# Scores of 64 rows filled up, gates summed in two parts, queries and keys turned

## The chip, the cores and the metric

The kernel runs on one core of one Trainium2 chip. The metric is device time in microseconds (us) of one execution; three runs are given, and their median counts. Every time in this document that is said to come from the profile belongs to one further execution, which a hardware profiler recorded. The engines are TensorE (PE; its weight loads are listed as PEld), VectorE (DVE), ScalarE (ACT), GpSimd (POOL) and SyncE (SP), whose queue issues nearly all transfers.

## The reference

256 tokens of width 2048 pass through three layers, all in fp32.

- **Retention** (8 heads, 256 wide queries and keys, 512 wide values): `h = rmsnorm(x) * (1 + scale) + shift`, where shift, scale and gate are `silu(c) @ ada_w + ada_b`; `proj = h @ w_in` (2048 x 12288) gives q, k, v and g; q and k are rotated by the positions (half-split rotary embedding over all 256 columns); scores `q k^T` times a decay, times v, normalised per head, times `silu(g)`, `@ w_out`; `x = x + gate * y`.
- **Latent attention** (16 heads): again shift, scale and gate; low-rank q and kv; each head's score is a product over 128 plain columns plus one over 64 rotated columns, whose key is the same for all heads; softmax, values, gate.
- **Mixed attention and experts**: 16 forgetting heads of 64 columns, whose score gets a difference of cumulated log gates added; 16 dilated heads of 64 columns, of which 16 are rotated; then a PEER layer with 16384 experts: each token's top experts weigh a down and an up projection.

## The kernel before

**Products in three parts.** A big fp32 product is done as three products of type fp32r, whose elements are a high part `h` and a low part `l = x - h`: high times high, high times low, low times high, all summed in PSUM. `split` (L169) makes the parts: ACT copies to the high part (L170), DVE subtracts (L171). Weights come by `weights` (L173): one DMA of 1 MB into one of three `raw` buffers, then two half tiles, each split into one of four pairs of buffers. Small products (scores, values, the gates' sums) are plain fp32, which PE runs as two records each.

**Projections.** `proj_steps` (L228) computes 256 tokens x 512 columns: for each of the 16 blocks of 128 input columns and for each half `tb` of the tokens, the activations (128 x 128) are the stationary operand and the weights (128 x 512) the moving one; three matmuls (L241 to L243). After each half weight tile it yields, and `proj` calls `tick` (L199), which advances background tasks at set rates: attention of the head pair before, transposes, the adaptive sums of the next layer. So the program order is fixed by Python; the framework's planner then orders the instructions of each engine by its own model of when operands are ready, and that order is fixed on the chip.

**Retention.** `begin` (L550) starts before all of the normalised input is there: ten column blocks are done in four quarters `g` of the input columns and summed up in SBUF, those of q and k of the first head pair among them. `angles` (L390) makes the tables of cosines and sines, tokens on the partitions. Then head pairs 1 to 3 follow (`project`, L606). The evacuation of q and k (L633) rotates the PSUM result with `rope` (L519: four DVE products, two POOL sums), and since the score needs q and k with their columns on the partitions, four PE transposes per 128 tokens follow (L640), and an ACT copy (L641). `attend` (L656) runs later, beside the next projections.

**Gates.** `ada_gate` (L478) computes four gate blocks of 512 columns for a layer: DVE sums 16 weight rows per partition into `acc` (L432, four DMA loads of 1 MB; one load is one step of the task), and PE sums over the partitions and spreads the result to all of them:

```
            nc.tensor.matmul(p, self.ones, acc, start=True, stop=False)
            nc.tensor.matmul(p, self.ones[0:1, :], bias[0:1, :], start=False, stop=True)
```

The task runs at 0.3 (layer 0) and 0.32 (layer 1) steps per tick; `output` (L703) calls `upto`, which runs the task until the gates that its column block needs are done.

**Scores.** `softmax_v` (L325) does one head: for each half of the queries the score products (L337), mask and maximum, exponential, transposes (L352), values (L358 to L360). In the latent heads a score is two products, the second over 64 rows (L857): the rotated parts of two heads lie in rows 0 to 63 and 64 to 127 of `qrT`, and `krT` holds the key twice. In the mixed attention the forgetting heads have 66 rows (64 and two for the cumulated gates), the dilated heads 64 (`kk`, L977 and L1028).

Of the kernel before, what the change touches and what calls it, by code (L numbers as in the profile page):

```python
# [36 lines left out]
C_ID, C_ONE, C_TRI, C_IOTA, C_CAUSAL, C_DIL, C_COS2, C_SIN2, C_INVF, C_END = (  # L37
    0, 128, 256, 384, 512, 768, 1152, 1168, 1184, 1312)
# [8 lines left out]
def shape_constants():  # L47
    c = np.zeros((128, C_END), np.float32)
    i = np.arange(128)
    c[:, C_ID:C_ID + 128] = np.eye(128)  # L50
    c[:, C_ONE:C_ONE + 128] = 1.0
    c[:, C_TRI:C_TRI + 128] = i[:, None] <= i[None, :]
    c[:, C_IOTA:C_IOTA + 128] = i[None, :]
    c[:, C_CAUSAL + 128:C_CAUSAL + 256] = np.where(i[None, :] <= i[:, None], 0.0, NEG)

    def dil(q, k):
        d = q[:, None] - k[None, :]
        n = ((d >= 0) & (d <= 128)).astype(np.int64)
# [11 lines left out]
    c[:, C_INVF:C_INVF + 128] = np.float32(10000.0) ** (-np.arange(0, 256, 2, dtype=np.float32) / np.float32(256))  # L70
# [52 lines left out]
class Net:  # L123
# [131 lines left out]

    def columns_steps(self, out, pool, name, nk, src, gain=None, shift=None, bufs=1, tiles=None, pause=False):
# [108 lines left out]
    def start(self):  # L365
# [19 lines left out]
        self.ones = self.cst[:, C_ONE:C_ONE + 128]  # L385
        nc.scalar.dma_start(self.cst, a["consts"])
# [3 lines left out]
    def angles(self):  # L390

        nc, keep, a = self.nc, self.keep, self.a
        self.cos = keep.tile([128, 2, 128], F32, name="cos")
        self.sin = keep.tile([128, 2, 128], F32, name="sin")
        pi = keep.tile([128, 2], I32, name="posi")
        nc.scalar.dma_start(pi, a["positions"].rearrange("o (b p) -> p (o b)", p=128))
        pf = keep.tile([128, 2], F32, name="posf")
        nc.vector.tensor_copy(pf, pi)
        ang = self.w(256).rearrange("p (b f) -> p b f", b=2)
        for tb in range(2):  # L400
            nc.vector.tensor_scalar(ang[:, tb, :], self.cst[:, C_INVF:C_INVF + 128], pf[:, tb:tb + 1], None,
                                    op0=OP.mult)
        k = self.w(256).rearrange("p (b f) -> p b f", b=2)
# [10 lines left out]
        nc.scalar.activation(self.sin, ang, AF.Sin)  # L414
        nc.vector.scalar_tensor_tensor(k, ang, -1.0, ang, op0=OP.mult, op1=OP.max)
        nc.vector.tensor_scalar(k, k, -1.0, float(np.pi / 2), op0=OP.mult, op1=OP.add)
        nc.scalar.activation(self.cos, k, AF.Sin)
# [60 lines left out]
    def ada_gate(self, layer, G):  # L478

        nc = self.nc  # L480
        for g in range(4):
# [52 lines left out]
    def retention(self):  # L534
# [5 lines left out]
        with self.phase("ret", 8), self.tc.tile_pool(name="ret", bufs=1) as pool:  # L540
# [9 lines left out]
            def begin():  # L550
# [18 lines left out]
                for g in range(4):  # L569
                    ada = self.ada_first(g + 1, A, B, ring, acc) if g < 3 else iter(())  # L570
                    if g == 3:
                        self.angles()
                    for i, (c0, dst) in enumerate(blocks):
# [6 lines left out]
                        for _ in self.proj_steps(ps, hT[g:], 4 * g, 4, w_in, c0, 512):  # L580
                            pass
# [24 lines left out]
            def project(i, between=None):  # L606
# [18 lines left out]
                def product(c0, early, ev):  # L625
                    if early is not None:
                        for tb in range(2):
                            ev(tb, early[:, tb, :])
                    else:
                        self.proj(hT, 0, 16, w_in, c0, 512, ev)  # L630

                for n, dst in enumerate((qT, kT)):
                    def ev(tb, p, dst=dst):  # L633
                        o = self.w()
                        self.rope(p.rearrange("p (h s d) -> p h s d", h=2, s=2),
                                  o.rearrange("p (h s d) -> p h s d", h=2, s=2), 2, 128,
                                  self.cos[:, tb, :], self.sin[:, tb, :])
                        p2 = self.tmp()
                        for j in range(4):
                            nc.tensor.transpose(p2[:, j * 128:j * 128 + 128], o[:, j * 128:j * 128 + 128], self.ident)  # L640
                        nc.scalar.activation(dst[:, :, tb * 128:tb * 128 + 128],  # L641
                                             p2.rearrange("p (k t) -> p k t", k=4), AF.Copy)
                    product(n * 2048 + i * 512, None if qk is None else qk[:, :, n * 512:n * 512 + 512], ev)
                for b in range(2):
                    def ev(tb, p, b=b):
                        nc.scalar.activation(v[:, tb, b * 512:b * 512 + 512], p, AF.Copy)
                    if i > 1:
                        product(4096 + i * 1024 + b * 512, None, ev)
# [91 lines left out]
    def latent(self):  # L740
# [4 lines left out]
        with self.phase("mla", 7), ExitStack() as es:  # L745
# [18 lines left out]
            krT = pool.tile([128, 256], F32, name="krT")  # L764
# [3 lines left out]
            def latents():  # L768
# [18 lines left out]
                nc.scalar.activation(krT, p[:, :256], AF.Copy)  # L787
# [5 lines left out]
            for c0, c1 in ((0, 424), (424, 848), (848, 1272), (1272, 1696), (1696, 2112)):  # L793
                def ev(tb, p, c0=c0, c1=c1):
                    o = max(64 - c0, 0)
                    if o:
                        self.rope(p[:, :64].rearrange("p (h s d) -> p h s d", h=1, s=2), kr[:, tb], 1, 32,
                                  self.cos[:, tb, ::4], self.sin[:, tb, ::4])
# [12 lines left out]
            def project(i):  # L811
# [6 lines left out]
                def evq(tb, p):  # L818
# [5 lines left out]
                              self.cos[:, tb, ::4], self.sin[:, tb, ::4])  # L824
# [20 lines left out]
            def head(i, j):  # L845
# [3 lines left out]
                def done(o, rd):  # L849
                    nc.vector.tensor_scalar(rd, rd, 0.5, None, op0=OP.mult)  # L850
                    for tb in range(2):
# [5 lines left out]
                                (qrT[j * 64:j * 64 + 64, tb * 128:tb * 128 + 128],  # L857
                                 krT[j * 64:j * 64 + 64, :128 * (tb + 1)])],
# [70 lines left out]
    def mixed(self):  # L929
# [3 lines left out]
        with self.phase("mix", 8), self.tc.tile_pool(name="mix", bufs=1) as pool:  # L933
# [41 lines left out]
            def project(n, g, beside=iter(())):  # L975

                kk = 66 if n == "f" else 64  # L977
# [16 lines left out]
                for off in (0, 1024):  # L994
                    def ev(tb, p, off=off):
# [15 lines left out]
                        else:  # L1011
                            nc.scalar.activation(dst[:, 0, :, 16:64], pv[:, :, 16:64], AF.Copy,
# [4 lines left out]
                        for h in range(0, 8, 4):  # L1017
                            p2 = self.tmp()
                            for j in range(4):
                                nc.tensor.transpose(p2[:kk, j * 128:j * 128 + 128], dst[:, 0, h + j, :kk], self.ident)  # L1020
                            nc.scalar.activation(dT[:kk, h:h + 4, tb * 128:tb * 128 + 128],
                                                 p2[:kk, :].rearrange("p (h t) -> p h t", h=4), AF.Copy)
# [3 lines left out]
            def head(n, g, h):  # L1026
                qT, kT, v = st[n, g]
                kk = 66 if n == "f" else 64  # L1028
# [6 lines left out]
                def done(o, rd):  # L1035
# [5 lines left out]
                    lambda tb: [(qT[:kk, h, tb * 128:tb * 128 + 128], kT[:kk, h, :128 * (tb + 1)])],  # L1041
# [538 lines left out]
```

## Time and profile before

| | us |
|---|---|
| median of three runs (3292.64 to 3299.68) | 3298.16 |
| profiled execution, its own time | 3290.79 |
| its span in the trace | 3289.0 |
| PE busy | 3199.2 (97%) |
| PE weight loads busy | 2731.8 (83%) |
| DVE busy | 2366.5 (72%) |
| ACT busy | 1563.5 (48%) |
| POOL busy | 403.9 (12%) |

705.51 MB are moved, 215 GB/s on average. The granted clock of PE is 0.996 over the execution. A matmul's record is longer than its distance to the next one, since matmuls overlap; so the start times in a timeline tell what one costs, and the busy share doesn't.

### The profile page before, as it was taken

The page shows a single profiled execution, that of the slowest core. Times are in us where ns is not written, and L with a number is a line of the kernel's source. Part 1 is how long each engine was busy: PE and PEld are TensorE (multiplying, and loading weights), DVE is VectorE, ACT ScalarE, POOL GpSimd, SP SyncE. Part 2 cuts the span into 40 slices and gives each one's busy share as a digit, 9 for nine tenths or more (in the row PEclk, how much of TensorE's full clock was granted, in tenths as well). Part 3 has the DMA queues.
Part 4 walks back from the last instruction along what each step waited for, and adds up shares of the span by engine and source line. Part 5 has one row for each costly group of instructions (what it writes and reads, how often), then busy time and mean ns, then how long its engine had stood idle before and what let it go on. Part 6 is the DMA issues. An engine that isn't in the chain of part 4 may idle for free.

```text
span 3289.0 us, 46220 instructions
## 1 busy us (share of the span) xinstructions
PE 3199.2 (97%) x17874; PEld 2731.8 (83%) x17874; DVE 2366.5 (72%) x3923; ACT 1563.5 (48%) x2167; POOL 403.9 (12%) x478
## 2 busy tenths in 40 slices
PE   5999999999999999999999999999999999999998
PEld 3777778777788878887787999999888898999987
DVE  6898778778786666455569976999766666566665
ACT  3544444343545546555454444555544444444444
POOL 0001101101000230000000221788000000000000
PEclk9999999999999999999999999999999999999999
DMA  9875677676575334443454456777977755555553
GB/s 343 315 259 204 222 282 293 235 272 255 194 282 202 127 144 171 154 149 135 147 173 152 167 180 212 238 259 248 317 240 240 240 208 204 198 200 192 192 192 141
DMA packets 141532, 705.51 MB, mean 215 GB/s; under 512 B 12664, under 2 KB 45688, under 8 KB 67584
## 3 DMA queue, kind: packets, MB, share of 16 engines
q1 hardware_dynamic: 139152, 696.51, 60.2%
q10 hardware_dynamic: 2160, 6.05, 0.5%
q8 instruction: 140, 2.29, 0.3%
q14 instruction: 80, 0.66, 0.1%
HBM read 676.30 MB, written 26.21 MB: 214 GB/s over the span
## 4 chain that ended last, share of the span: by engine, by line
PE 80%; DVE 10%; DMA 5%; issue 3%; ACT 1%; POOL 1%; POOLq 0%; DVEq 0%; SPq 0%; ACTq 0%
PE acc L241 12%; PE acc L242 12%; PE acc L243 11%; PE acc L1249 7%; PE acc L1251 7%; PE acc L1250 7%; PE tmp L1169 5%; PE tmp L1170 5%; PE tmp L1171 5%; DVE wl L171 3%; PE tmp L337 2%; DVE w L432 1%; PE acc L1171 1%; PE acc L1170 1%; PE acc L1169 1%
## 5 line engine op out<-in xcount | busy, mean ns | idle before, releaser
L171 DVE TENSOR_TENSOR wl<-raw,wh 128x1024 fp32r<-128x1024 f32 (+4 forms) x983 | 1202.3, 1229 | 504.1 <-ACT wh L170 503.0
L170 ACT ACTIVATE wh<-raw 128x1024 fp32r<-128x1024 f32 (+4 forms) x983 | 1017.5, 1043 | 1008.0 <-PE acc L243 383.3
L242 PE MATMUL acc<-wl,hTh 128*128 128x512 f32 (+4 forms) x1536 | 599.7, 391 | 11.1 <-DVE wl L171 11.1
L241 PE MATMUL acc<-wh,hTh 128*128 128x512 f32 (+4 forms) x1536 | 604.2, 396 | 2.1 <-ACT wh L170 2.0
L243 PE MATMUL acc<-wh,hTl 128*128 128x512 f32 (+4 forms) x1536 | 597.6, 389 | 0.7 <-DVE hTl L288 0.7
L1169 PE MATMUL tmp<-hTh,wh 128*128 128x256 f32 x1280 | 360.6, 282 | 0.0
L1170 PE MATMUL tmp<-hTh,wl 128*128 128x256 f32 x1280 | 357.9, 280 | 0.0
L1171 PE MATMUL tmp<-hTl,wh 128*128 128x256 f32 x1280 | 357.3, 279 | 0.0
L242 PEld LDWEIGHTS acc<-wl,hTh 128*128 128x128 f32 x1536 | 290.4, 189 | 74.8 <-DVE wl L171 17.7
L241 PEld LDWEIGHTS acc<-wh,hTh 128*128 128x128 f32 x1536 | 289.6, 189 | 63.6 <-ACT wh L170 4.5
L243 PEld LDWEIGHTS acc<-wh,hTl 128*128 128x128 f32 x1536 | 289.8, 189 | 62.4 <-issue 2.4
L1249 PE MATMUL acc<-wh,Wh 128*128 128x512 f32 x812 | 317.1, 390 | 0.3 <-ACT Wh L170 0.2
L1251 PE MATMUL acc<-wh,Wl 128*128 128x512 f32 x812 | 316.3, 390 | 0.9 <-DVE Wl L171 0.9
L1250 PE MATMUL acc<-wl,Wh 128*128 128x512 f32 x812 | 316.2, 389 | 0.0
L1169 PEld LDWEIGHTS tmp<-hTh,wh 128*128 128x128 f32 x1280 | 240.5, 188 | 0.7
L1170 PEld LDWEIGHTS tmp<-hTh,wl 128*128 128x128 f32 x1280 | 240.0, 188 | 0.8
L1171 PEld LDWEIGHTS tmp<-hTl,wh 128*128 128x128 f32 x1280 | 240.0, 188 | 0.1
L1467 POOL TENSOR_SCALAR oh<-iota,slot 128x128 f16<-128x128 f16 x256 | 209.6, 837 | 167.8 <-DVE iota L1458 87.1
L432 DVE SCALAR_TENSOR_TENSOR w<-raw,cact,w 128x512 f32<-128x512 f32 x240 | 183.1, 763 | 18.3 <-DMA raw<-in_ada_dram 13.7
L160 POOL TENSOR_TENSOR tiny<-tiny,mhalf 128x1 f32<-128x1 f32 (+1 forms) x23 | 17.6, 764 | 1382.5 <-DVE tiny L159 1382.5
L1170 PE MATMUL acc<-hTh,wl 128*128 128x256 f32 x640 | 179.9, 281 | 6.8 <-DVE wl L171 6.8
L1249 PEld LDWEIGHTS acc<-wh,Wh 128*128 128x128 f32 x812 | 152.4, 188 | 33.7 <-DVE x L1258 2.3
(352 smaller groups left out, 5220.2 us busy)
## 6 DMA issues: line engine op xcount, KB each, us to landing
raw<-in_down_dram SPq DMA_DIRECT2D x128, 1024.0 KB, 5.3
raw<-in_up_dram SPq DMA_DIRECT2D x128, 1024.0 KB, 4.9
raw<-in_ret_w_in_dram SPq DMA_DIRECT2D x96, 1024.0 KB, 5.5
raw<-in_ada_dram SPq DMA_DIRECT2D x64, 1024.0 KB, 5.6
raw<-in_w_in_dram SPq DMA_DIRECT2D x44, 1024.0 KB, 4.8
raw<-in_ret_w_out_dram SPq DMA_DIRECT2D x32, 1024.0 KB, 4.8
G<-in_ada_first_dram SPq DMA_DIRECT2D x32, 512.0 KB, 5.1
raw<-in_mla_w_out_dram SPq DMA_DIRECT2D x16, 1024.0 KB, 4.8
```

The costliest lines, as they stand in the source:

```text
L170: self.nc.scalar.activation(h, raw, AF.Copy)
L171: self.nc.vector.tensor_tensor(l, raw, h.bitcast(F32), op=OP.subtract)
L241: nc.tensor.matmul(o, sh, wh[:, j, :], start=(k == 0), stop=False)
L242: nc.tensor.matmul(o, sh, wl[:, j, :], start=False, stop=False)
L243: nc.tensor.matmul(o, sl, wh[:, j, :], start=False, stop=(k == nk - 1))
L432: nc.vector.scalar_tensor_tensor(acc, r, self.cact[:, k:k + 1], acc, op0=OP.mult, op1=OP.add)
L1169: nc.tensor.matmul(o, dh[:, s], hh[:, k % 4, :], start=(k == 0), stop=False)
L1170: nc.tensor.matmul(o, dl[:, s], hh[:, k % 4, :], start=False, stop=False)
L1171: nc.tensor.matmul(o, dh[:, s], hl[:, k % 4, :], start=False, stop=(k == 15))
L1249: nc.tensor.matmul(y[tb][c], Wh[:, s], uh[:, u], start=first, stop=False)
L1250: nc.tensor.matmul(y[tb][c], Wh[:, s], ul[:, u], start=False, stop=False)
L1251: nc.tensor.matmul(y[tb][c], Wl[:, s], uh[:, u], start=False, stop=last)
```

## The change

- **Scores.** `krT` gets one plane per head of a pair, with the key in that head's 64 rows and zeros in the others; the product takes all 128 rows of `qrT`. The dilated heads get two columns of zeros behind their 64, and 66 rows take part everywhere.
- **Gates.** The bias is added to row 0 of `acc`; `acc` is split in a high and a low part, and two fp32r products with a tile of ones follow, one step later. A gate is five steps instead of four, and `output` asks for them so.
- **Queries and keys.** `turned_steps` makes the weights (128 x 128) the stationary operand and the activations (128 x 256 tokens) the moving one, so that q and k arrive with their columns on the partitions: half a head (128 columns) in each half of a PSUM bank. They are rotated straight from there (four DVE products of 512 columns, four POOL sums of 256 per block of two heads) into `qT` and `kT`; the transposes and their copies are gone. `angles` makes tables with the columns on the partitions, and small ones (32 columns) of the old form for the latent layer.

```diff
+    def turned_steps(self, ps, hT, nk, name, c0):
+        nc = self.nc
+        k = 0
+        for k0 in range(hT[0], hT[0] + nk, 4):
+            for wh, wl in self.weights(name, k0, c0):
+                for j in range(2):
+                    hh, hl = (t[:, (k0 + k % 4) % 4, :] for t in hT[1][(k0 + k % 4) // 4])
+                    for c in range(4):
+                        o = ps[c // 2][:, c % 2 * 256:c % 2 * 256 + 256]
+                        sh, sl = (t[:, j, c * 128:c * 128 + 128] for t in (wh, wl))
+                        nc.tensor.matmul(o, sh, hh, start=(k == 0 and c % 2 == 0), stop=False, skip_group_check=True)
+                        nc.tensor.matmul(o, sh, hl, start=False, stop=False, skip_group_check=True)
+                        nc.tensor.matmul(o, sl, hh, start=False, stop=(k == nk - 1 and c % 2 == 1),
+                                         skip_group_check=True)
+                    k += 1
+                yield
...
     def ada_gate(self, layer, G):
...
-            p = self.tmp()
             bias = self.w()
             nc.scalar.dma_start(bias[0:1, :], self.a["ada_b"][layer:layer + 1, c0:c0 + 512])
-            nc.tensor.matmul(p, self.ones, acc, start=True, stop=False)
-            nc.tensor.matmul(p, self.ones[0:1, :], bias[0:1, :], start=False, stop=True)
+            nc.vector.tensor_tensor(acc[0:1, :], acc[0:1, :], bias[0:1, :], op=OP.add)
+            ah, al = (self.w().bitcast(F32R) for _ in range(2))
+            self.split(acc, ah, al)
+            yield
+            p = self.tmp()
+            nc.tensor.matmul(p, self.onesr, ah, start=True, stop=False)
+            nc.tensor.matmul(p, self.onesr, al, start=False, stop=True)
...
-                        for _ in self.proj_steps(ps, hT[g:], 4 * g, 4, w_in, c0, 512):
+                        if i < 2:
+                            steps = self.turned_steps(ps, (4 * g, hT), 4, w_in, c0)
+                        else:
+                            steps = self.proj_steps(ps, hT[g:], 4 * g, 4, w_in, c0, 512)
+                        for _ in steps:
                             pass
...
+                    if qk is None:
+                        ps = [self.acc() for _ in range(2)]
+                        for _ in self.turned_steps(ps, (0, hT), 16, w_in, n * 2048 + i * 512):
+                            self.tick()
+                    for h in range(2):
+                        p = (ps[h] if qk is None else qk[:, h, n * 512:n * 512 + 512]).rearrange(
+                            "p (s t) -> p s t", s=2)
+                        t = [self.w().rearrange("p (s t) -> p s t", s=2) for _ in range(2)]
+                        for o, tab in zip(t, (self.cosT, self.sinT)):
+                            nc.vector.tensor_tensor(o, p, tab[:, None, :].to_broadcast([128, 2, 256]), op=OP.mult)
+                        nc.gpsimd.tensor_tensor(dst[:, 2 * h, :], t[0][:, 0, :], t[1][:, 1, :], op=OP.subtract)
+                        nc.gpsimd.tensor_tensor(dst[:, 2 * h + 1, :], t[0][:, 1, :], t[1][:, 0, :], op=OP.add)
...
-                    self.upto(ada, 4 * cb + 4)
+                    self.upto(ada, 5 * cb + 5)
...
-            krT = pool.tile([128, 256], F32, name="krT")
+            krT = pool.tile([128, 2, 256], F32, name="krT")
+            nc.gpsimd.memset(krT, 0.0)
...
-                nc.scalar.activation(krT, p[:, :256], AF.Copy)
+                for d in range(2):
+                    r = slice(d * 64, d * 64 + 64)
+                    nc.scalar.activation(krT[r, d, :], p[r, :256], AF.Copy)
...
-                                (qrT[j * 64:j * 64 + 64, tb * 128:tb * 128 + 128],
-                                 krT[j * 64:j * 64 + 64, :128 * (tb + 1)])],
+                                (qrT[:, tb * 128:tb * 128 + 128], krT[:, j, :128 * (tb + 1)])],
...
+                            nc.gpsimd.memset(dst[:, 0, :, 64:66], 0.0)
...
-                    lambda tb: [(qT[:kk, h, tb * 128:tb * 128 + 128], kT[:kk, h, :128 * (tb + 1)])],
+                    lambda tb: [(qT[:66, h, tb * 128:tb * 128 + 128], kT[:66, h, :128 * (tb + 1)])],
```

## Rows read from the trace of the kernel before

**Rows 1.** The page's first part: busy us, share of the span, instructions of each engine.
```profile
PE 3199.2 (97%) x17874; PEld 2731.8 (83%) x17874; DVE 2366.5 (72%) x3923; ACT 1563.5 (48%) x2167; POOL 403.9 (12%) x478
```

**Rows 2.** Stretches (us): length, then busy us of each engine; clock, DMA share, GB/s.
```profile
274.00:858.00 584.00, 569.83 (x2480) 446.89 (x2479) 461.49 (x619) 238.63 (x285) 67.21 (x64) 0.99 0.68 250
858.00:1012.00 154.00, 147.61 (x704) 128.75 (x703) 124.05 (x177) 72.33 (x110) 4.48 (x6) 0.98 0.73 264
1012.00:1258.00 246.00, 245.48 (x1259) 200.84 (x1258) 163.66 (x373) 128.48 (x265) 51.76 (x57) 1.00 0.40 136
1258.00:1600.00 342.00, 338.38 (x1711) 273.37 (x1709) 176.52 (x409) 186.73 (x330) 10.33 (x30) 1.00 0.45 157
```

**Rows 3.** PE's waits: line, waited for whom: us in total, times, longest.
```profile
PE acc L242 <- DVE wl L171: 12.6, 14, 3.0
...
PE tmp L640 <- POOL w L530: 10.3, 6, 5.4
```

**Rows 4.** PE's timeline in a projection: start us, us, line, operation, shapes, count.
```profile
270.12 0.40 PE L243 MATMUL acc<-wh,hTl 128*128 128x512 f32 x1
...
284.12 0.40 PE L243 MATMUL acc<-wh,hTl 128*128 128x512 f32 x1
```

**Rows 5.** PE's timeline around a score of 66 rows and one of 64 rows.
```profile
1333.62 0.40 PE L243 MATMUL acc<-wh,hTl 128*128 128x512 f32 x1
1333.86 0.39 PE L337 MATMUL tmp<-qkT,qkT 66*128 66x128 f32 x2
...
1334.32 0.40 PE L242 MATMUL acc<-wl,hTh 128*128 128x512 f32 x1
...
1506.29 0.39 PE L242 MATMUL acc<-wl,hTh 128*128 128x512 f32 x1
1506.61 0.48 PE L337 MATMUL tmp<-qkT,qkT 64*128 64x128 f32 x2
...
1507.37 0.39 PE L241 MATMUL acc<-wh,hTh 128*128 128x512 f32 x1
```

**Rows 6.** Line L337 on PE: count, ns min/median/max, first and last start, forms.
```profile
L337 PE MATMUL tmp<-qkT,qkT x128: 272/375/481, 1333.9 to 1645.2; 66*128 66x128 f32 x32, 66*128 66x256 f32 x32, 64*128 64x128 f32 x32, 64*128 64x256 f32 x32
...
L337 PE MATMUL tmp<-krT,qrT x64: 272/374/480, 1033.0 to 1213.7; 64*128 64x128 f32 x32, 64*128 64x256 f32 x32
```

**Rows 7.** Groups in 274 to 858: busy us, mean ns | idle before, releaser.
```profile
L432 DVE SCALAR_TENSOR_TENSOR w<-raw,cact,w 128x512 f32<-128x512 f32 x180 | 138.1, 767 | 14.9 <-DMA raw<-in_ada_dram 11.5
...
L516 DVE TENSOR_TENSOR w<-acc,G 128x512 f32<-128x512 f32 x30 | 19.6, 683 | 0.8 <-PE acc L243 0.8
...
L528 DVE TENSOR_TENSOR w<-acc,cos 128x256 f32<-128x256 f32 x24 | 9.9, 413 | 0.1
...
L530 POOL TENSOR_TENSOR w<-w 128x256 f32<-128x256 f32 x12 | 9.1, 762 | 42.7 <-DVE w L529 42.7
```

**Rows 8.** PE's timeline at a gate, and line L490 as a whole.
```profile
336.72 1.02 PE L490 MATMUL tmp<-w,cst 128*128 128x512 f32 x2
337.67 1.12 PE L491 MATMUL tmp<-w,cst 1*128 1x512 f32 x2
338.72 1.09 PE L273 MATMUL tmp<-ident,sg 128*128 128x128 f32 x8
...
L490 PE MATMUL tmp<-w,cst x16: 590/592/667, 336.7 to 1003.9; 128*128 128x512 f32 x16
```

**Rows 9.** PE's timeline in the experts' down projection.
```profile
1849.96 0.28 PE L1170 MATMUL acc<-hTh,wl 128*128 128x256 f32 x1
...
1852.78 0.28 PE L1170 MATMUL acc<-hTh,wl 128*128 128x256 f32 x1
```

**Rows 10.** The page's groups: weight loads of the down projection.
```profile
L1169 PEld LDWEIGHTS tmp<-hTh,wh 128*128 128x128 f32 x1280 | 240.5, 188 | 0.7
```

**Rows 11.** PE's timeline at the first head pair's transposes.
```profile
285.05 1.91 PE L640 MATMUL tmp<-ident,w 128*128 128x128 f32 x16
```

**Rows 12.** PE's timeline at the longest wait, and the stretch behind it.
```profile
630.59 0.48 PE L640 MATMUL tmp<-ident,w 128*128 128x128 f32 x1 [5.39 <-POOL w L530]
...
630.00:634.00 4.00, 3.41 (x12) 2.77 (x13) 4.00 (x7) 0.03 (x1) 3.04 (x4) 0.58 0.15 23
```

More of the change, by code (lines that the diff above doesn't have):

```diff
@@ L69, in shape_constants @@
         c[:, C_SIN2 + 8 * b:C_SIN2 + 8 * b + 8] = np.sin(ang[b * 128:b * 128 + 128].astype(np.float64))
-    c[:, C_INVF:C_INVF + 128] = np.float32(10000.0) ** (-np.arange(0, 256, 2, dtype=np.float32) / np.float32(256))
+    freq = np.float32(10000.0) ** (-np.arange(0, 256, 2, dtype=np.float32) / np.float32(256))
+    c[:, C_INVF:C_INVF + 32] = freq[::4]
+    c[:, C_COLF] = freq
     m = np.zeros((128, 8, 384), np.float32)
@@ L385, in start, with angles, trig @@
         self.ones = self.cst[:, C_ONE:C_ONE + 128]
+        self.onesr = keep.tile([128, 128], F32R, name="onesr")
         nc.scalar.dma_start(self.cst, a["consts"])
         nc.vector.tensor_scalar(self.colv[:, V_GN:V_GN + 32], self.colv[:, V_GN:V_GN + 32], 0.5, None, op0=OP.mult)
-    def angles(self):
+    def angles(self, pool):
         nc, keep, a = self.nc, self.keep, self.a
-        self.cos = keep.tile([128, 2, 128], F32, name="cos")
-        self.sin = keep.tile([128, 2, 128], F32, name="sin")
+        self.cosT = pool.tile([128, 256], F32, name="cosT")
+        self.sinT = pool.tile([128, 256], F32, name="sinT")
+        self.cos = keep.tile([128, 2, 32], F32, name="cos")
+        self.sin = keep.tile([128, 2, 32], F32, name="sin")
+        pos = a["positions"]
+        pr = self.w(256).bitcast(I32)
+        nc.scalar.dma_start(pr, bass.AP(tensor=pos.tensor, offset=pos.offset, ap=[[0, 128], [1, 256]]))
+        ang = self.w(256)
+        nc.vector.tensor_copy(ang, pr)
+        nc.vector.tensor_scalar(ang, ang, self.cst[:, C_COLF:C_COLF + 1], None, op0=OP.mult)
+        self.trig(ang, self.cosT, self.sinT, 256)
+        nc.vector.tensor_copy(self.onesr, self.ones)
         pi = keep.tile([128, 2], I32, name="posi")
-        nc.scalar.dma_start(pi, a["positions"].rearrange("o (b p) -> p (o b)", p=128))
+        nc.scalar.dma_start(pi, pos.rearrange("o (b p) -> p (o b)", p=128))
         pf = keep.tile([128, 2], F32, name="posf")
         nc.vector.tensor_copy(pf, pi)
-        ang = self.w(256).rearrange("p (b f) -> p b f", b=2)
+        ang = self.w(64)
         for tb in range(2):
-            nc.vector.tensor_scalar(ang[:, tb, :], self.cst[:, C_INVF:C_INVF + 128], pf[:, tb:tb + 1], None,
-                                    op0=OP.mult)
-        k = self.w(256).rearrange("p (b f) -> p b f", b=2)
+            nc.vector.tensor_scalar(ang[:, tb * 32:tb * 32 + 32], self.cst[:, C_INVF:C_INVF + 32], pf[:, tb:tb + 1],
+                                    None, op0=OP.mult)
+        self.trig(ang, *(t.rearrange("p b f -> p (b f)") for t in (self.cos, self.sin)), 64)
+    def trig(self, ang, cos, sin, n):
+        nc = self.nc
+        k = self.w(n)
         magic = 12582912.0
@@ L623, in project @@
                             nc.scalar.activation(v[:, tb, b * 512:b * 512 + 512], early["v"][b][:, tb, :], AF.Copy)
[L625 to L630, printed above, removed]
-                for n, dst in enumerate((qT, kT)):
[L633 to L643, printed above, removed]
+                for n, dst in enumerate((qT, kT)):
+                    if qk is None:
[10 more added lines that the diff above has]
+                        nc.gpsimd.tensor_tensor(dst[:, 2 * h + 1, :], t[0][:, 1, :], t[1][:, 0, :], op=OP.add)
                 for b in range(2):
@@ L647, in project @@
                     if i > 1:
-                        product(4096 + i * 1024 + b * 512, None, ev)
+                        self.proj(hT, 0, 16, w_in, 4096 + i * 1024 + b * 512, 512, ev)
                 if between:
@@ L1019, in ev @@
                             for j in range(4):
-                                nc.tensor.transpose(p2[:kk, j * 128:j * 128 + 128], dst[:, 0, h + j, :kk], self.ident)
-                            nc.scalar.activation(dT[:kk, h:h + 4, tb * 128:tb * 128 + 128],
-                                                 p2[:kk, :].rearrange("p (h t) -> p h t", h=4), AF.Copy)
+                                nc.tensor.transpose(p2[:66, j * 128:j * 128 + 128], dst[:, 0, h + j, :], self.ident)
+                            nc.scalar.activation(dT[:66, h:h + 4, tb * 128:tb * 128 + 128],
+                                                 p2[:66, :].rearrange("p (h t) -> p h t", h=4), AF.Copy)
                     self.proj(hT, 0, 16, w_in, base + off + g * 512, 512, ev)
```

16 lines of the change are left out of this document (7 added, 9 removed).

## The prediction

> **What bounds the kernel now.** I read four views in this order. First the page: TensorE (PE) shows 97% busy [rows 1]; a matmul's record overlaps the next one, so this alone proves little. Second, the windows by stage: the reader sees the retention stage (274 to 858 us), the latent projections (858 to 1012), the latent heads (1012 to 1258) and the mixed attention (1258 to 1600) with PE busy 570 of 584, 148 of 154, 245 of 246 and 338 of 342 us, the clock at 0.98 to 1.00 (the 2.4 GHz level), VectorE (DVE) at 79%, 81%, 67% and 52% [rows 2]. Third, the waits: PE waits in all only 12.6 us for split weights (L242) and 10.3 us for rotated queries and keys that it is to transpose (L640) [rows 3]. Fourth, PE's timeline, start to start, since only the spacing of matmuls says what they cost. A stream of 512-column products, each with its own weight load, starts 60 in 14.00 us, 0.2333 us apart [rows 4]. So in the four stages that the change touches PE issues almost without a pause: what leaves PE's stream shortens the time, and what enters it lengthens it, as long as DVE and the weight buffers keep up.
>
> **Scores with 64 rows.** Both are fp32 score products of L337. In the forgetting heads (66 rows, 128 columns) the way from the product before to the second product after is 1334.32 - 1333.62 = 0.70 us; in the dilated heads (64 rows, same columns) it is 1507.37 - 1506.29 = 1.08 us [rows 5]. Less the two 512-column products inside, 0.47 us, the block costs 0.23 and 0.61 us. The 0.38 us are idle time at the change from a full-height product to a 64-row one and back; the streamed columns are the same. The blocks: 64 records in the dilated heads (half of the 128 of qkT) and 64 of the latent heads' krT [rows 6], two records to a block, so 32 and 32. Going through the timeline I count 32 separate runs of krT and 28 of the dilated heads (four blocks follow another directly and share the change). 60 x 0.38 = 22.8 us. The change makes them 66 and 128 rows. That 66 rows run without the pause is in the row; that 128 rows do is what every projection shows. Bounds: 0 if zero rows bring nothing, 22.8 if all is gone. I take 22.8; nothing else is late there, since PE is busy 99.8% and 99% of these stretches while DVE has a third or more free [rows 2]. Added: eight small POOL fills, one fill for krT and one more ScalarE (ACT) copy, ahead of transposes or projections that wait on other engines; I cost them at nothing, and at most the 0.76 us of a 256-column POOL row [rows 7] for each of the nine fills, 7 us, if POOL became late.
>
> At this place a rule of the Trainium skill speaks against the change: in TensorE: Matmul & The Clock Gate, section "Part 3: Packing small matmuls", products of few rows that lie in different row groups run side by side in the array, so filling them up to the full height gives that up. Two heads' krT products do lie in rows 0 to 63 and 64 to 127. By that rule half of the 32 krT blocks would be free today, about 0.34 us each, and the gain would be 5 us smaller. The trace disagrees: each of the 32 stands alone between projections.
>
> **Gates.** A gate's sum is now two fp32 products of 512 columns (two records each), the second with one row. From the first to what follows: 338.72 - 336.72 = 2.00 us; there are 16 records, so 8 gates, four in each layer [rows 8]. After: two single-pass products, 2 x 0.2333 = 0.47 us. 8 x 1.53 = 12.2 us less on PE. Bounds: a single-pass product with this stationary tile isn't shown; between 0.2333 us each and the 0.5 us of today's passes, so 8 to 12.2 us; I take 12.2, since every other product of this type has that spacing. Added on DVE: a one-row sum and a subtraction of 512 columns, 0.69 us each at most [rows 7], 8 x 1.4 = 11 us; before the product stands a new step, so that other PE work covers them. Without cover it would cost 2 to 3 us a gate.
>
> The extra step also moves the background schedule. Layer 0's task advances 0.3 steps per half weight tile. By my count it has done 17 steps when the first output's last block asks for 20 (before: 16 are asked, and done by then). Three steps then come at once: two 1 MB loads in SP's queue ahead of that block's weights, and 8 sums of 0.77 us on DVE, 6.1 us [rows 7], ahead of its weight splits. PE has up to four split halves (11 us) in hand. Between 0 and 8 us; I take 3. The later column sums end about three ticks later (164 for 161 of 176), still before the stage's end: nothing. In layer 1 the last gate slips into the heads, where DVE has room: nothing.
>
> **Queries and keys.** Eight projections (two done by quarters in the first stage, six whole ones later) go from 96 products of 512 columns to 192 of 256, with the weights stationary. The down projection has this very form: from 1849.96 to 1852.78 are 24 starts, 0.1175 us each [rows 9]. 192 x 0.1175 - 96 x 0.2333 = 0.16 us; eight projections, +1.3 us. Bounds: 0.1167 (half of 0.2333) and, if a load of 188 ns were not hidden, 0.188 [rows 9, 10]. I take 0.1175, the nearest row.
>
> Removed: 64 PE transposes, 16 of them in 1.91 us [rows 11], 7.6 us in all; the 10.3 us of waits for POOL [rows 3]; and the clock's fall after the longest of them, 5.39 us at 625: the granted clock of 630 to 634 is 0.58, so mostly at the 1.2 GHz level, where 4 us do the work of 2.3 [rows 12], 1.7 us lost. Together 19.6 us. The rotation itself stays: DVE takes four 512-column products in place of eight of 256, 4 x 0.69 for 8 x 0.41 us [rows 7], a little less; POOL has the same four, and ACT is rid of 16 copies. It is now late for the scores instead of the transposes; these come four half tiles, some 11 us, after the projection, and the chain is about 2.8 us of DVE and two POOL pieces of under 1 us: covered, unless DVE is late by 6 us. The tables cost DVE some 3 us more in the first stage, beside PE's work: nothing.
>
> **The sum.** -22.8 - 12.2 - 19.6 + 1.3 + 3 = -50.3 us. In retention PE would run some 5% faster, and DVE (79% busy, with a split that follows ACT's and a DMA) will not always keep up: 4 us given back, a fifth of what the retention stage gains; this is an estimate from its 12.6 us of waits. Net -46 us. The profiled execution took 3290.79 us (span 3289.0 and 1.8 around it): 3245 us. The median of the runs, 3298.16, lies 7.4 us above it, which would give 3252; I forecast the middle, 3248 us.
>
> **Rivals.** (a) The weights run late: the planner's order puts a wait elsewhere, in retention and the latent projections, and of 19.6 and 12.2 us only a third is kept, with the scores' 22.8. For: DVE at 79 and 81%, a forced triple step. Against: PE waits for weights only 12.6 us today. Gain 22.8 + 10.6 - 4.3 = 29 us: 3265.
> (b) The fill doesn't remove the pause (it does not do what it says: the pause comes from somewhere else than the height). For: the two kinds of heads differ in masks too. Against: idle starts right at the change of height, in both stages. Gain 46 - 23 = 23 us: 3271.
> (c) Slower: the weight load of the turned products shows. 8 x 192 = 1536 products at 0.188 in place of 0.1175 us: +108 us, so 62 us more than before: about 3356. It decides from a spacing of 0.1175 + 46/1536 = 0.147 us. For: nothing in the projections shows a fresh weight tile as the stationary one. Against: the down projection does, 6144 times, at 0.1175. The Trainium skill has the rule for it (the same page, "What overlaps and what doesn't": a weight load overlaps running products only in another row group); by that rule all products here would pay for their loads, and the trace's 0.1175 us between full-height products whose loads are recorded with 0.188 us disagrees.
>
> **Chances.** Forecast 0.71, its own range 3232 to 3262; (a) 0.14, in 0.03 of it with all of its gain gone; (b) 0.06; (c) 0.06; the rest, 0.03, a gain over 65 us. The range 3225 to 3274 takes in (a) and (b). A measurement here can tell 0.2%, 6.6 us, from no change. Faster 0.91, same 0.03, slower 0.06.
>
> **What would show it.** The scores: L337's 64-row forms gone, start to start as in the 66-row rows, no idle "issue" before them. The gates: two products 0.23 us apart. The turned blocks: 256-column forms with a spacing of 0.118; above 0.147 I am wrong. L640 absent, and no new PE wait of more than 5 us in retention; a wait for the weights near 440 to 480 us would be the forced steps. Wrong also if PE's waits for L171 double.

## The result and the profile after

The changed kernel takes 3251.92 us (median of 4 runs, 3248.29 to 3254.39); the kernel before, run beside it, 3296.32 us (3292.64 to 3299.68). The ratio is 0.9865, with a 95% interval from 0.9853 to 0.9878: 40 to 49 us less. The forecast was 3248 us, range 3225 to 3274. The profiled execution took 3252.83 us (span 3251.0), 38.0 us less than the one before (3290.79): that one lay 5.5 us under the median of its kernel, this one 0.9 over. Differences of rows below add up to 38, not to 44.

The page's first part after, as [rows 1] had it before:

```profile
PE 3159.2 (97%) x18562; PEld 2762.0 (85%) x18562; DVE 2366.0 (73%) x3918; ACT 1558.4 (48%) x2162; POOL 414.4 (13%) x487
```

The same four stretches as in [rows 2], moved to where they now lie (length; busy us of PE, PEld, DVE, ACT, POOL; clock, DMA share, GB/s):

```profile
276.00:841.00 565.00, 557.02 (x2989) 469.09 (x2988) 463.93 (x605) 232.80 (x273) 77.61 (x64) 0.99 0.71 260
841.00:988.00 147.00, 140.12 (x694) 126.91 (x693) 119.18 (x172) 71.88 (x111) 4.07 (x7) 0.99 0.72 255
988.00:1228.00 240.00, 237.39 (x1262) 200.55 (x1261) 170.31 (x387) 130.29 (x271) 52.45 (x57) 1.00 0.44 153
1228.00:1564.00 336.00, 332.88 (x1711) 274.65 (x1711) 175.77 (x409) 186.47 (x329) 11.20 (x38) 1.00 0.46 160
```

The reader sees more matmuls in less time (the turned products are half as wide), DVE's work unchanged (2366.0 us) and so a little denser. PE's waits, for [rows 3]: the one for rotated queries and keys (10.3 us) is gone, the one for split weights grew from 12.6 to 15.6 us.

```profile
PE acc L244 <- DVE wl L173: 15.6, 16, 3.0
```

In PE's timeline the three parts look as follows. First a score in the dilated heads, the very block of [rows 5] that began at 1506.61: now 66 rows, and from the product before to the second behind it 1476.77 - 1476.01 = 0.76 us in place of 1.08 (0.69 in most of the blocks of this size). Then line L359's forms: no 64 is left (compare [rows 6]).

```profile
1476.01 0.40 PE L244 MATMUL acc<-wl,hTh 128*128 128x512 f32 x1
1476.25 0.45 PE L359 MATMUL tmp<-qkT,qkT 66*128 66x128 f32 x2
1476.45 0.48 PE L245 MATMUL acc<-wh,hTl 128*128 128x512 f32 x1
1476.77 0.39 PE L243 MATMUL acc<-wh,hTh 128*128 128x512 f32 x1
...
L359 PE MATMUL tmp<-qkT,qkT x128: 272/356/484, 1303.3 to 1604.6; 66*128 66x128 f32 x64, 66*128 66x256 f32 x64
...
L359 PE MATMUL tmp<-krT,qrT x64: 275/328/380, 1014.2 to 1183.7; 128*128 128x128 f32 x32, 128*128 128x256 f32 x32
```

Then a gate, between turned products: its two products take 346.01 - 345.55 = 0.46 us of PE, for the 2.00 us of [rows 8]. And turned products later: 24 distances from start to start between 598.04 and 600.87, 0.118 us each, as in [rows 9], each with its own weight load.

```profile
345.43 0.28 PE L273 MATMUL acc<-hTh,wl 128*128 128x256 f32 x1
345.55 0.39 PE L534 MATMUL tmp<-w,onesr 128*128 128x512 f32 x1
345.78 0.40 PE L535 MATMUL tmp<-w,onesr 128*128 128x512 f32 x1
346.01 0.28 PE L271 MATMUL acc<-hTh,wh 128*128 128x256 f32 x1
...
598.04 0.28 PE L271 MATMUL acc<-hTh,wh 128*128 128x256 f32 x1
...
600.87 0.28 PE L271 MATMUL acc<-hTh,wh 128*128 128x256 f32 x1
```

To see where the time came from, I summed the distance from each matmul's start to the next one's, stretch by stretch, and within a stretch by what the matmul computes; a wait is then counted with the matmul ahead of it.

| stretch of PE's stream | before | after | difference | forecast |
|---|---|---|---|---|
| first instruction to first projection | 43.9 | 48.0 | +4.1 | 0 |
| to retention's last projection | 814.3 | 792.9 | -21.4 | -17.4 |
| to the end of latent attention | 393.3 | 380.2 | -13.1 | -18.3 |
| to the end of mixed attention | 452.1 | 441.7 | -10.5 | -10.6 |
| experts, to the end | | | +3.0 | 0 |
| profiled execution | 3290.79 | 3252.83 | -38.0 | -46 |

(The forecast's terms sorted into the stretches: four gates, 6.1 us, in each of the first two stages; 32 x 0.38 = 12.2 us of scores in the latent heads, 28 x 0.38 = 10.6 in the dilated ones; 19.6 - 1.3 - 3 - 4 in retention.)

### The profile page after: what moved, and what is told of

Read it like the earlier page. It is cut to its first block, busy times and chain, and to the rows that moved or that the text cites. A ratio compares the mean times of both kernels' runs of the same rounds, so it can differ in the third digit from the quotient of the medians.

```text
span 3251.0 us, 47605 instructions
## 1 busy us (share of the span) xinstructions
PE 3159.2 (97%) x18562; PEld 2762.0 (85%) x18562; DVE 2366.0 (73%) x3918; ACT 1558.4 (48%) x2162; POOL 414.4 (13%) x487
## 4 chain that ended last, share of the span: by engine, by line
PE 83%; DVE 8%; DMA 4%; issue 3%; ACT 1%; POOL 0%; SPq 0%; DVEq 0%; POOLq 0%; ACTq 0%
PE acc L244 11%; PE acc L245 11%; PE acc L243 11%; PE acc L1294 7%; PE acc L1296 7%; PE acc L1295 7%; PE tmp L1214 5%; PE tmp L1216 5%; PE tmp L1215 5%; DVE wl L173 3%; PE acc L272 2%; PE acc L273 2%; PE acc L271 2%; PE tmp L359 1%; PE acc L1214 1%
## 5 line engine op out<-in xcount | busy, mean ns | idle before, releaser
L244 PE MATMUL acc<-wl,hTh 128*128 128x512 f32 (+4 forms) x1280 | 497.4, 389 | 13.1 <-DVE wl L173 13.1
L243 PE MATMUL acc<-wh,hTh 128*128 128x512 f32 (+4 forms) x1280 | 498.3, 391 | 1.5 <-ACT wh L172 1.5
L245 PE MATMUL acc<-wh,hTl 128*128 128x512 f32 (+4 forms) x1280 | 496.7, 388 | 0.0
L244 PEld LDWEIGHTS acc<-wl,hTh 128*128 128x128 f32 x1280 | 241.8, 189 | 63.1 <-DVE wl L173 18.4
L245 PEld LDWEIGHTS acc<-wh,hTl 128*128 128x128 f32 x1280 | 241.8, 189 | 47.9 <-DVE hTl L310 0.4
L243 PEld LDWEIGHTS acc<-wh,hTh 128*128 128x128 f32 x1280 | 241.2, 189 | 46.5 <-ACT wh L172 1.7
```

The lines of the kernel that those rows point to most:

```text
L243: nc.tensor.matmul(o, sh, wh[:, j, :], start=(k == 0), stop=False)
L244: nc.tensor.matmul(o, sh, wl[:, j, :], start=False, stop=False)
L245: nc.tensor.matmul(o, sl, wh[:, j, :], start=False, stop=(k == nk - 1))
```

## Experiments: the three parts alone

Each kernel is the one before with one part of the change. All were timed beside the kernel before (3295.8 us).

```diff
-            krT = pool.tile([128, 256], F32, name="krT")
+            krT = pool.tile([128, 2, 256], F32, name="krT")
... (and the dilated heads' two columns of zeros)
```

> The kernel before with the fill of the 64-row scores alone. Theory (each of 60 changes of height costs 0.38 us of pause): 22.8 us faster than before, 12.2 of it in the latent heads (32 changes) and 10.6 in the mixed attention (28). Rival one, from the changed kernel's trace, where the latent heads gained only 6.5 us: the heads are held by the evacuation of their projections too, the gain there is about 6.5 and the whole 17 us. Rival two (the pause has another cause than the height): no gain.

Measured: 3279.39 us, ratio 0.9945 (0.9931 to 0.9960): 13 to 23 us less, against 22.8 forecast. The middle, 18 us, is nearer to rival one (17). By rows the pause itself is gone: the key's products (krT) fell from 16.7 to 6.8 us, the plain part beside them from 13.4 to 11.8, the mixed scores (qkT) from 22.9 to 14.0, and the whole mixed stretch is 10.8 us shorter. But the latent stretch is only 1.9 us shorter (391.4 for 393.3). There the heads' projections and transposes took 2.9 us more, as rival one had it, and the latent projections ahead of them 6.9 us more: PE waited 3.0 us for a split at 995.8, and behind a gate's products its granted clock was 0.66 between 910 and 915, so mostly at the 1.2 GHz level (1.00 in the kernel before). This profile is of the longest of six executions (3268.48 to 3282.25), so what the latent stretch gains in the others isn't shown.

```diff
-            nc.tensor.matmul(p, self.ones, acc, start=True, stop=False)
-            nc.tensor.matmul(p, self.ones[0:1, :], bias[0:1, :], start=False, stop=True)
...
+            self.split(acc, ah, al)
+            yield
...
+            nc.tensor.matmul(p, self.onesr, ah, start=True, stop=False)
+            nc.tensor.matmul(p, self.onesr, al, start=False, stop=True)
```

> The kernel before with the gates in two parts alone. Theory: 8 x 1.53 us less on PE and 3 us (0 to 8) given back by three steps that are forced at once before the first output's last block: 9 us faster. Rival: the forced steps and the work added on VectorE take all of it: within 2 us of before. In the trace: the time from the first product to what follows falls from 2.0 to 0.47 us in either case; waits of PE between 440 and 500 us are the forced steps.

Measured: 3280.94 us, ratio 0.9957 (0.9945 to 0.9968): 10 to 18 us less, more than the 12.2 - 3 of my terms. A part of the surplus is in the next section: the longest wait of [rows 12] is gone here too (0.98 us for 5.39).

```diff
-                        for _ in self.proj_steps(ps, hT[g:], 4 * g, 4, w_in, c0, 512):
+                        steps = self.turned_steps(ps, (4 * g, hT), 4, w_in, c0)
... (for q and k; rotation from PSUM, no transposes)
```

> The kernel before with queries and keys turned alone (and their tables). Theory: 19.6 us of transposes, waits and low clock go, 1.3 us come: 18 us faster, with retention's first product at 44 us as before. Rival: the planner's new order of the first loads (a weight load ahead of the adaptive ones, the first product 4.1 us later in the changed kernel) belongs to this part: 14 us faster, first product at 48 us. Second rival, weight loads of the turned products show: slower by up to 90 us.

Measured: 3289.57 us, ratio 0.9982 (0.9974 to 0.9991): only 3 to 9 us less. This is a third of what I had put on this part. In the place of the 5.39 us wait for the rotation (625.2 to 630.6, [rows 12]) PE now waits for a step of layer 1's adaptive sums, whose DVE instruction L511 stands in its queue behind the rotation and three weight splits:

```profile
629.30 3.49 DVE L173 TENSOR_TENSOR wl<-raw,wh 128x1024 fp32r<-128x1024 f32 x3
...
632.78 0.15 DVE L511 SCALAR_TENSOR_TENSOR tiny<-tmp,colv 128x2 f32<-128x2 f32 x1
...
632.98 1.87 PE L506 MATMUL tmp<-cst,w 128*128 128x1 f32 x8 [4.03 <-DVE tiny L511]
```

The parts alone add up to 18 + 14 + 6 = 38 us by their ratios, all three together to 44.5 (40 to 49). The difference lies within the intervals.

## Experiments: whose wait was it?

My first theory was that the late sums ate the turned part's gain when it stands alone, and that it is worth 12 us beside the other two.

```diff
-                            steps = self.turned_steps(ps, (4 * g, hT), 4, w_in, c0)
+                        for _ in self.proj_steps(ps, hT[g:], 4 * g, 4, w_in, c0, 512):
... (the changed kernel with queries and keys as before)
```

> The kernel before with the filled scores and the summed gates, queries and keys as before. Theory (the turned part alone gave only 6 us because a late adaptive sum took the place of the wait for the rotation, and the earlier gates' slack changes that): 3296 - 18 - 14 = 3264 us, so that the turned part is worth 12 us beside the other two. Rival (the parts add up, and turned is worth 6 us in either kernel): 3258 us.

Measured: 3259.37 us beside 3295.63, ratio 0.9890 (0.9873 to 0.9906). The rival's figure: the turned part is worth some 7 to 8 us here too.

The next two leave out layer 1's shift and scale sums (loads and DVE's multiplications; zeros stand in their place), in the kernel before and in the one with the turned part alone.

```diff
+        if layer == 1 and c0 < 2 * D:
+            nc.vector.memset(acc, 0.0)
+            for kg in range(4):
+                yield
+            return
```

> The kernel before without layer 1's shift and scale sums (their loads and VectorE's multiplications left out, zeros in their place). It is the base for the run after it. The column sums that TensorE makes of them stay. Expected 3270 to 3297 us: nothing on TensorE is removed but waits for these sums.

> The kernel with the turned queries and keys alone, without layer 1's shift and scale sums as in the run before it. Theory: the turned part alone gave 6 us and not 18 because the adaptive sums' loads and VectorE's work for them ended late and TensorE waited 4.3 us for them at 640 us; without them it is 14 to 18 us faster than the run before. Rival: the sums are not the reason, the turned products or the start cost more than thought: 4 to 8 us faster than the run before.

Measured: 3279.97 and 3274.13 us, ratios to the kernel before 0.9958 (0.9944 to 0.9972) and 0.9932 (0.9915 to 0.9948). The pair differs by 6 to 9 us (with an uncertainty of some 5), not by 14 to 18. My theory fell. What the traces show instead: without the sums the long wait is gone from the kernel that still transposes, and so it is with the new gates alone. PE's timeline at the same transposes, with the rotation's first product on DVE, in the kernel before without the sums, and then in the one with the gates alone:

```profile
618.66 0.42 DVE L533 TENSOR_TENSOR w<-acc,cos 128x256 f32<-128x256 f32 x1
...
621.02 0.33 PE L645 MATMUL tmp<-ident,w 128*128 128x128 f32 x1 [0.84 <-POOL w L535]
```

```profile
626.08 0.42 DVE L534 TENSOR_TENSOR w<-acc,cos 128x256 f32<-128x256 f32 x1
...
628.38 0.33 PE L647 MATMUL tmp<-ident,w 128*128 128x128 f32 x1 [0.98 <-POOL w L536]
```

In the kernel before, DVE's timeline shows what the rotation stood behind. The last product of the projection starts at 621.30 and the first rotation product at 628.23, 6.9 us later. In between DVE does a weight split, two statistics and a gating product of the attention beside it, and three sums of layer 1 (2.3 us):

```profile
622.53 1.21 DVE L171 TENSOR_TENSOR wl<-raw,wh 128x1024 fp32r<-128x1024 f32 x1
...
624.85 0.75 DVE L432 SCALAR_TENSOR_TENSOR w<-raw,cact,w 128x512 f32<-128x512 f32 x1
...
626.77 1.53 DVE L432 SCALAR_TENSOR_TENSOR w<-raw,cact,w 128x512 f32<-128x512 f32 x2
628.23 0.41 DVE L528 TENSOR_TENSOR w<-acc,cos 128x256 f32<-128x256 f32 x1
```

The same distance is 0.75 us without the sums (617.91 to 618.66) and 2.8 us with the gates alone (623.27 to 626.08), and from the first rotation product to the first transpose it is 2.3 to 2.4 us in all three. So the profile names POOL's rotation as the releaser, but the lateness was that of DVE's queue ahead of it. The sums are a third of that queue and not all of it: with the gates alone sums still stand there, and the attention's work came earlier. The second longest wait for the rotation, 2.90 us at 378.5, came before layer 1's sums had begun (the last gate of layer 0 is summed at 471), and it too fell to 1.04 and 0.67 us in these two kernels. A kernel without transposes meets a late queue at its next wait for DVE (the 4.03 us above). In the changed kernel the waits for that step are 0.4 us in retention, and without the gates' extra step they are back (next section). What the turned part brings by itself, in the pair without sums: from the first retention score (294.8 and 296.9) to retention's last projection (844.6 and 836.3) 549.8 and 539.4 us, so 10.4 us, of which the 48 transposes in this stretch took 4.1 and their waits 4.9 (the other 16, 1.7 us, lie ahead of it); 2.1 us are lost ahead of it, in the first stage.

## Experiments: cover, rates, height, start

**The extra step as cover.** The changed kernel without the step between a gate's split and its products.

```diff
-            yield
             p = self.tmp()
...
-                    self.upto(ada, 5 * cb + 5)
+                    self.upto(ada, 4 * cb + 4)
```

> The changed kernel with the extra step of a gate taken out: sum, split and both products come in one step, and a gate is four steps as before, so nothing is forced at once. Theory one (the step is what covers the bias sum and the split, 2 us of VectorE and ScalarE): PE waits about 2 us at each of 8 gates, 16 us, and the forced steps' waits (6.8 us of gaps between 475 and 498 us in the changed kernel) go: about 9 us slower than the changed kernel, 36 us faster than before. Theory two (the planner puts other PE work in front anyway, and the forced steps are the price of the extra step): about 5 us faster than the changed kernel, 49 us faster than before.

Measured: 3262.63 us (3260.72 to 3274.41), ratio 0.9902 (0.9887 to 0.9916) for the changed kernel's 0.9865: some 11 us slower, near theory one's 9. PE stands at a gate, and waits for layer 1's sums come back (the third figure is the longest):

```profile
PE tmp L533 <- ACT w L172: 5.6, 2, 5.4
PE tmp L508 <- DVE tiny L513: 5.1, 3, 3.4
```

So the step does cover the split, but my price without it, 2 to 3 us a gate, was wrong in kind: one gate cost 5.4 us, most cost next to nothing. The rest came with the changed order of the background, which this run changes along with the cover: the waits for the sums in the second row, and 10.6 us more in the latent projections (151.6 for 141.0), in a profile of the longest of the four executions.

**Rates.** Other rates for the gates' tasks, so that no step is forced in the output projection and the last gate doesn't slip into the latent heads.

```diff
-ADA_RATE = 0.3
+ADA_RATE = 0.34
...
-            gate = self.later(self.ada_gate(1, G), 0.32)
+            gate = self.later(self.ada_gate(1, G), 0.4)
```

> The changed kernel with ADA_RATE 0.34 for 0.3 and layer 1's gate at 0.4 for 0.32, so that no sum is forced in the output projection's step and the last gate ends ahead of the latent heads. Theory: what the changed kernel lost against the forecast in these two places is the planner's, about 2 to 4 us in the forced steps at 475 to 498 us and 0.6 to 2 us in the latent heads, so 3247 to 3250 us. Rival: the sums only move, and VectorE's work for them delays evictions elsewhere by as much: 3251 to 3255 us.

Measured: 3254.91 us (3246.79 to 3256.46), ratio 0.9869 (0.9853 to 0.9886): no difference, as the rival said. Its mechanism is in the rows. The forced steps' waits are gone from 476 to 497 us. In latent attention three rows of the heads' projections and transposes got 3.0 us shorter (ident,w 12.2 to 11.5, cqTl 12.9 to 11.7, ckvTl 17.7 to 16.6), and the projections ahead of them 4.6 longer (the hTh and hTl products, 141.0 to 145.6).

**Height.** The changed kernel with the forgetting heads' scores over 64 rows; the two rows with the cumulated gates are left out.

```diff
+                kk = 64 if n == "f" else 66
...
-                    lambda tb: [(qT[:66, h, tb * 128:tb * 128 + 128], kT[:66, h, :128 * (tb + 1)])],
+                    lambda tb: [(qT[:kk, h, tb * 128:tb * 128 + 128], kT[:kk, h, :128 * (tb + 1)])],
```

> The changed kernel with the forgetting heads' scores over 64 rows in place of 66 (the two rows with the cumulated gates are left out). Nothing else differs: same products, same columns, same instructions. Theory (a change between full height and 64 rows costs 0.38 us wherever it occurs): about 28 to 32 new pauses, 10.6 to 12 us slower than the changed kernel, all of it in the mixed attention's stretch, in the spacing behind the score products. Rival (the pause of the dilated heads came from their mask or their data, not from the height): no change, within 2 us.

Measured: 3261.09 us beside the changed kernel's 3253.27 on the same chip (ratios 0.9896 and 0.9875): 7 to 8 us slower, less than the theory's 10.6 to 12, and the intervals overlap. But the mixed stretch, where the edit is, takes 451.6 for 441.5 us, +10.1, and the scores in it 22.9 for 14.1; the rest of this execution was 3.3 us shorter. In its timeline a forgetting head has what the dilated ones had before: 1303.19 - 1302.11 = 1.08 us.

```profile
1302.11 0.40 PE L245 MATMUL acc<-wh,hTl 128*128 128x512 f32 x1
1302.44 0.49 PE L359 MATMUL tmp<-qkT,qkT 64*128 64x128 f32 x2
1302.86 0.50 PE L243 MATMUL acc<-wh,hTh 128*128 128x512 f32 x1
1303.19 0.40 PE L244 MATMUL acc<-wl,hTh 128*128 128x512 f32 x1
```

Mask and data are those of the heads that had no pause: the height alone makes it. The Trainium skill has the rule, without a price (TensorEngine Tiling (Array Packing), "Key Properties": changing the tiling mode drains TensorE; its "Available Configurations" list 64 rows as a mode of their own). The trace agrees for 64 rows among 128 (1.08 us a block), and blocks of 66 rows, at 0.69 to 0.76 us, don't show it.

**Start.** In the changed kernel SP issues the second weight load at 27.10 us (before: 40.08), and its two splits stand on DVE ahead of the adaptive sums on which the first projection waits:

```profile
36.38 1.23 DVE L173 TENSOR_TENSOR wl<-raw,wh 128x1024 fp32r<-128x1024 f32 x1 [2.27 <-ACT wh L172]
...
38.72 1.22 DVE L173 TENSOR_TENSOR wl<-raw,wh 128x1024 fp32r<-128x1024 f32 x1
...
45.99 0.16 DVE L515 TENSOR_TENSOR A<-tiny,colv 128x2 f32<-128x2 f32 x1
```

The experiment puts the load behind the adaptive sums' loads again.

```diff
...
+        if self.guard is not None:
+            self.nc.vector.tensor_copy(raw[0:1, 0:1], self.guard[0:1, 0:1])
...
+                        self.guard = ring[2] if g == 0 and i == 1 else None
```

> The changed kernel with one added wait in the first stage: the second projection's weight load waits (by a one-element copy) for a late load of the adaptive sums, so that it stands behind them in SP's queue again, as in the kernel before. Theory (the 4.1 us by which the first projection starts later in the changed kernel come from that load and its split ahead of the adaptive sums): the first product is 4 us earlier, at about 44 us, and the kernel 2 to 4 us faster than the changed one. Rival (the second projection then waits for its weights, or the gain is given back by the end of the first stage): first product at 44 us, but the first retention score no earlier than in the changed kernel, and the time within 1.5 us of it.

> The changed kernel once more, beside the two runs before it on the same chip: 3250 to 3254 us.

Measured: 3250.99 us (3250.76 to 3252.82) and 3253.27 (3249.42 to 3255.53), ratios 0.9871 (0.9856 to 0.9887) and 0.9875 (0.9858 to 0.9891). The first product is back at 44.3 us, but then waits for what was put back:

```profile
59.03 0.58 PE L273 MATMUL acc<-hTh,wh 128*128 128x256 f32 x1 [4.93 <-ACT wh L172]
```

The first retention score comes at 298.3 us for 297.5: the rival's first half holds. Whether the whole is 0 or 2 us faster can't be told from these runs. No experiment gave a version clearly ahead of the changed kernel.

## Why the prediction was right, and where its terms were not

- **Scores, -22.8: right.** By rows -11.9 in the latent heads (krT 16.7 to 6.9, kT 13.4 to 11.7, the transposes of the softmax weights 4.3 to 3.9), and the mixed stretch is 10.5 shorter (8.8 of it in the score products themselves). The fill on POOL and the extra copy cost nothing that shows in the mixed stretch. Rival (b) is out, by the height experiment. The rule on packed products that the prediction set against this term was not put to the test by the trace: no two of the krT blocks lie side by side, so its condition never occurs.
- **Gates, -12.2: right.** The lines took 8.0 + 7.6 us and take 2.1 + 2.0: -11.5, with 0.46 us at the gate shown and 0.51 on average for the 0.47 worked out.
- **Transposes, waits and clock, -19.6: the mis-sized term.** All 64 transposes took 6.0 us, not the 7.6 that I worked out from the first 16. Of the waits (10.3 us) the longest, 5.39 us, and the clock's fall behind it (1.7 us) hung on the queue on DVE and not on the transposes as such: they go with the gates' new steps alone, and when layer 1's sums alone are left out. In the sum this did little harm, as 18.0 of the 19.6 us go either way; the turned part by itself is worth 6 to 9 us, not 18.
- **Turned products, +1.3: right**; 0.118 us apart. Rival (c) is out.
- **Forced steps, +3 (0 to 8): in the range, but nearer 6.** PE waits for the weights in the forecast place and just behind it, five times between 476 and 497 us, 5.6 us in all; the same waits come with the gates alone, and are gone at the other rates. The longest:

```profile
476.55 0.73 PE L243 MATMUL acc<-wh,zTh 128*128 128x512 f32 x2 [1.23 <-ACT wh L172]
...
493.52 0.73 PE L243 MATMUL acc<-wh,hTh 128*128 128x512 f32 x2 [1.51 <-ACT wh L172]
...
496.34 0.79 PE L244 MATMUL acc<-wl,hTh 128*128 128x512 f32 x1 [2.10 <-DVE wl L173]
```

- **DVE's give-back, +4: nothing beyond the forced steps.** Waits for split weights (L244) grew by 3.0 us, but 2.9 of them are the forced steps' own, so the two terms, 7 us together, came to 5.6. Rival (a), a third of the gain, did not come: retention got 21.4 us shorter, and the longest new wait in it is the 2.10 us above.
- **The latent heads and the first stage, both put at nothing, cost some 4 us each.** The profile's missing 8 us are the latent stretch's 5.2 and 3.0 in the experts. In the experts no instruction was changed, and their stretch varies from 1585.1 to 1591.4 us in the traces here, so these 3.0 can't be put down to the change. The 4.1 us at the start are made up for by retention's 4.0 more than forecast. The latent stretch gained 17.6 us by its scores and gates, but the heads' projections and transposes took 4.7 more, with PE's longest waits there for the copies and the rotation of the latent queries, beside the last gate:

```profile
1000.86 0.44 PE L873 MATMUL tmp<-ident,w 128*128 128x128 f32 x2 [1.16 <-ACT w L867]
...
1004.72 0.33 PE L873 MATMUL tmp<-ident,w 128*128 128x128 f32 x1 [0.61 <-POOL w L575]
```

The gate that slipped is at most a part of it: with the scores alone, where no gate moved, the same rows took 2.9 us more, and with an earlier gate still 2.0. At the start 4.1 us were lost, of which the first stage returned 2.6: the first retention score is 1.5 us later than before. Why the order of SP's loads changed is open: it belongs to the turned part (first product at 47.5 us with it alone, 43.6 and 43.9 with the others), and the cause within it was not found.
- **From span to median:** the forecast of 3248 lay between the profiled execution's 3245 and the median's 3252. The median came out as the second. That it is only 4 us off is in part luck: the profiled executions differ by 38 us and the medians by 44, and the start, the latent heads and retention were each 4 to 5 us away from their forecasts, in both directions.

## What to carry to other kernels

Take a stage's cost from the distance between starts in PE's timeline, and price a change of height by comparing the same block in its two heights: by rows that term came out within 2% (22.4 us for 22.8). Before you credit an edit with a wait, look at what stood ahead of the releaser in its own queue; if other work there was late, the wait goes when that work moves, or comes back behind the next instruction that needs the engine. Where background sums share DVE and the loads with the weight splits, other rates for them can merely move the waits, as in the one try here. And before you read a stretch of one profile as the gain of an edit, compare that stretch in a second profile.

## What the runs showed of the chip

- Score products of 64 rows between products of 128 cost PE 10.1 to 10.8 us in the mixed stretch, where they form 28 separate runs: some 0.36 us each, whether the rows were filled up (10.5 and 10.8) or taken away (10.1). Products of 66 rows cost nothing of it.
- Products of 256 columns, each with a weight load that is recorded with 188 ns, start every 0.118 us. The load is hidden, also where the stationary operand is a freshly split weight tile.
- Layer 1's sums on DVE and their loads, with no matmul among them, cost the kernel before 9 to 18 us (ratio 0.9944 to 0.9972). In the trace retention is 13.2 us shorter without them; of that PE's waits for the rotation are 5.4, for split weights 3.0 and for the column sums 1.4. The run doesn't tell DVE's work from the loads.
